# Six of eight modulation blocks as vector sums on VectorE instead of matmuls on TensorE, and a fixed order for the first chunks

## The chip, the cores and the metric

The program runs on one core of one Trainium2 chip. The metric is the time of one execution in device microseconds (us); the median of several executions is given with the lowest and the highest. A profile is one further execution, taken by the hardware profiler.

## The reference

One layer of a diffusion backbone works on 256 latent tokens of width 1024, with 256 context tokens that serve only as keys and values. The part that matters here is the modulation: six vectors of 1024 (shift, scale and gate of two sublayers) come from one matrix of 1024 x 6144, applied to the conditioning vector.

```
mod = (silu(cond) @ w_mod + b_mod)                 # 1 x 6144
sh1, sc1, g1, sh2, sc2, g2 = split(mod, 6)
h = layer_norm(x); hc = layer_norm(ctx)
q, k, v, pool_in, ga, gb = split(modulate(h, sh1, sc1) @ w_in)
y_attn = softmax(q k^T / 8 + bias) v               # keys and values of the context too
y_pool = multiscale_pool(pool_in)
y = (sigmoid(ga) * (y_attn @ w_attn) + sigmoid(gb) * (y_pool @ w_pool)) @ w_out
h = layer_norm(alpha * h + g1 * y)
ffn = hierarchical_moe(modulate(h, sh2, sc2))      # 4 groups x 8 experts, 2 used per token
out = layer_norm(alpha * h + g2 * ffn)
```

modulate(h, sh, sc) is h * (1 + sc) + sh. All inputs are float32. The weights of 32 experts (gate, up and down, 2 MB each) are all streamed.

## The kernel before

**Stages.** The first stage normalises x (tiles xn0, xn1) and the context (xn2, xn3): `spread` (L184) makes a tile's mean and deviation on VectorE and ScalarE, `normalise` (L193) applies them, on VectorE for odd tiles and on ScalarE for even ones. Then a loop over k = 0 to 7 takes one chunk of 128 columns at a time. `modulation(k)` (L215) sums sh1 and sc1 of the chunk for c and for the context's vector: eight matmuls from sil (silu of both vectors) times wm, whose four groups of 32 output rows hold partial sums; VectorE copies them (pms, L226), and `modulation_columns` (L229) adds the four groups with a small matmul on selc, a matrix of ones at every 32nd row. `turn_x` transposes the chunk of xn on TensorE, `modulate` (L247) scales and shifts it on VectorE and splits it by `split` (L67) into a high part (copied on ScalarE) and a low part (subtracted on VectorE). `queries` and `keys` multiply it with split weights: `mm3` (L71) makes three matmuls of each product (high x high, high x low, low x high). So before every weight block, TensorE waits for one low part of VectorE. `wsplit` (L201) is the split of weights.

Then come scores and softmax (`scores` L369, `soft` L380; the softmax is on VectorE and ScalarE), the values (va, weights wvs), attention (po), the pooling branch (ua), the two branch gates (ga, 8 chunks with two halves each, weights wgs), the branch projections (pj, wps), w_out (oa, wos) with LayerNorm and router, and last the 32 experts with their streamed weights.

**Modulation blocks.** The other four vectors g1, sh2, sc2, g2 are columns 2048 to 6143 of w_mod. They are made in eight blocks n = 0 to 7 of 512 columns, two for each vector, scattered over the loops of the later stages. `mod_sum(n)` (L325) loads two tiles of 1 MB (wr), and makes eight matmuls, whose 32-row groups hold partial sums (pr); for g1 and g2 (n = 0, 1, 6, 7) a further matmul puts the bias row from gbt, a part of the tile g2b, in first (L330). ScalarE copies the result to ms. `mod_use` (L346) comes a few steps later in the loops. For n = 0, 1 it sums the groups and spreads them over 128 rows with one matmul (L343; selr is selc widened to 128 columns) into g1b. For n = 2 to 5 it makes columns: four matmuls with a part of ms as weights (L355), every fourth column of it, and VectorE adds biases and makes G2c and B2c, with which the router's weights are scaled (rw, L558, L559). The sums of n = 6, 7 are kept and spread after the router (L666).

In the value loop blocks 0 and 1 stand at k = 2 and 5, in attention blocks 2 and 3, in the gates blocks 4 and 5 at k = 1 and 5 of the first and block 6 at k = 2 of the second, in the projections block 7.

**What sets the order.** All engines work through their own queue in order. A tile scheduler places the instructions of the engines by data and priority, unless `keep_in_program_order` fixes them: `fx` does that for VectorE and ScalarE while early[0] holds, `fp` for TensorE while first[0] holds. All loads of weights go out on SyncE's queue in order, into a ring of eight 1 MB tiles ("big"; wm, wq, wr, wv, wu, wg, wp, wo), and the expert tiles, later also in the memory that earlier stages give back. A load whose tile is still in use holds the queue.

```
def split(hi, lo, src, low=None):
    fx(nc.scalar.copy(hi, src))
    fx((low or V).tensor_sub(lo, src, hi.bitcast(F32)))
```

## Time and profile before

| | before |
|---|---|
| median of 3 runs | 753.5 us (752.71 to 755.31) |
| profiled execution | 753.49 us |
| its span in the trace | 751.9 us |
| TensorE matmul busy | 586.5 us, 78% |
| VectorE busy | 280.4 us, 37% |
| ScalarE busy | 159.8 us, 21% |
| DMA | 260.10 MB, mean 346 GB/s |

The span runs from the first instruction to the last. Busy times are added over each engine and overlap with each other. A share of 78% is an average: which engine or queue limits a stage is seen only in the slices and windows of that stage.

### The profile page before, as it was taken

How to read it: one execution, taken by the hardware profiler on the slowest of the kernel's cores; microseconds unless marked ns; L12 is line 12 of the kernel's file. 1: busy time of each engine (PE TensorE's matmuls, PEld its weight loads, DVE VectorE, ACT ScalarE, POOL GpSimd, SP SyncE). 2: the span in 40 equal slices, each digit the busy share in tenths (PEclk: the TensorE clock that was granted, in tenths of full speed). 3: DMA queues.
4: the chain of work that ended last, by engine and by line, in shares of the span. 5: the costliest groups of instructions: out<-in, count | busy, mean ns of one | idle time of the engine just before them, and what ended most of it. 6: DMA issues, size and time to landing. Idle time of an engine off the chain costs nothing. (4 is left out here: it accounts for less than half of the span.)

```text
span 751.9 us, 16948 instructions
## 1 busy us (share of the span) xinstructions
PE 586.5 (78%) x7477; PEld 434.0 (58%) x7478; DVE 280.4 (37%) x726; ACT 159.8 (21%) x311; POOL 18.1 (2%) x41
## 2 busy tenths in 40 slices
PE   5799999999999998987667667676676576886463
PEld 3688665588899766865345435434443346663352
DVE  4568617633445864533112122112111242321036
ACT  4233435553553553101001001000000000000000
POOL 1000000000000012000000000000000010000003
PEclk8799999999999998999789788696886966989688
DMA  9999464477798874999999999999999999999992
GB/s 293 321 358 385 159 201 169 154 252 265 269 346 331 305 264 177 404 416 414 420 418 418 419 418 419 418 418 418 417 420 418 418 418 416 414 420 418 418 324 84
DMA packets 69629, 260.10 MB, mean 346 GB/s; under 512 B 6569, under 2 KB 27561, under 8 KB 45229
## 3 DMA queue, kind: packets, MB, share of 16 engines
q1 hardware_dynamic: 69550, 258.97, 88.8%
q8 instruction: 60, 0.98, 0.5%
q14 instruction: 19, 0.15, 0.0%
HBM read 257.90 MB, written 1.05 MB: 344 GB/s over the span
## 5 line engine op out<-in xcount | busy, mean ns | idle before, releaser
L752 PE MATMUL gue<-wgu,xgd 128*32 128x128 f32 x4096 | 171.3, 327 | 76.4 <-DMA wgu<-in_w_expert_up_dram 56.8
L752 PEld LDWEIGHTS gue<-wgu,xgd 128*32 128x32 f32 x4096 | 138.2, 131 | 113.6 <-DMA wgu<-in_w_expert_up_dram 68.1
L752 PE MATMUL ye<-wd,aTe 128*32 128x256 f32 x960 | 72.0, 431 | 37.9 <-DVE aTe L814 17.9
L826 DVE TENSOR_TENSOR yp<-ye,g2b 32x256 f32<-32x256 f32 x120 | 50.4, 420 | 88.9 <-PE ye L752 87.6
L803 ACT ACTIVATE sie<-gue 128x128 f32<-128x128 f32 x32 | 8.9, 278 | 329.6 <-PE gue L752 329.6
L809 DVE TENSOR_TENSOR spe<-gue,sie 128x128 f32<-128x128 f32 x32 | 12.0, 376 | 171.5 <-ACT sie L803 171.4
L752 PEld LDWEIGHTS ye<-wd,aTe 128*32 128x32 f32 x960 | 32.1, 120 | 65.5 <-issue 17.4
L752 PE MATMUL pdd<-OHd,hx 128*128 128x128 f32 x256 | 41.7, 312 | 4.1 <-DVE yp L826 3.8
L752 PEld LDWEIGHTS pdd<-OHd,hx 128*128 128x128 f32 x256 | 36.5, 219 | 14.1 <-issue 7.5
L752 PE MATMUL ya<-yp,OTg 128*128 128x512 f32 (+1 forms) x72 | 33.4, 595 | 7.0 <-DVE yp L826 5.8
L780 ACT ACTIVATE xgd<-pdd,B2c,G2c 128x128 f32<-128x128 f32 x32 | 14.7, 458 | 89.3 <-DVE xgd L782 86.7
L782 DVE TENSOR_SCALAR xgd<-pdd,G2c,B2c 128x128 f32<-128x128 f32 x32 | 13.1, 410 | 51.7 <-PE pdd L752 51.5
L752 PEld LDWEIGHTS ya<-yp,OTg 128*128 128x128 f32 x72 | 12.4, 196 | 21.7 <-DVE yp L826 13.9
L336 PE MATMUL pr<-wr,sil 128*32 128x512 f32 x128 | 15.4, 598 | 0.0
L388 ACT ACTIVATE sb<-sb,mx 128x512 f32<-128x512 f32 x16 | 11.4, 717 | 13.3 <-DVE mx L387 13.3
L397 PE MATMUL ptt<-ident,sb 128*128 128x128 f32 x64 | 10.2, 284 | 2.7 <-DVE yaT L69 2.4
L835 DVE COPY OTg<-potg 128x256 f32<-128x256 f32 x8 | 3.4, 425 | 21.2 <-PE ya L752 19.0
L397 PEld LDWEIGHTS ptt<-ident,sb 128*128 128x128 f32 x64 | 6.9, 140 | 6.8 <-DVE yaT L69 4.6
L918 POOL PARTITION_BROADCAST l<-l1r x4 | 2.8, 798 | 318.6 <-DMA wgu<-in_w_expert_up_dram 318.6
L443 PEld LDWEIGHTS po<-pT,kv 128*64 128x64 f32 x128 | 7.2, 136 | 5.6 <-ACT pT L399 2.4
L814 DVE STREAM_TRANSPOSE aTe<-spe 128x128 f32<-128x128 f32 x32 | 10.0, 311 | 1.1
L374 PE MATMUL s<-kv,qT 64*128 64x512 f32 x32 | 9.9, 639 | 0.5 <-DVE mx L386 0.5
(850 smaller groups left out, 977.3 us busy)
## 6 DMA issues: line engine op xcount, KB each, us to landing
wgu<-in_w_expert_gate_dram SPq DMA_DIRECT2D x64, 1024.0 KB, 19.9
wgu<-in_w_expert_up_dram SPq DMA_DIRECT2D x64, 1024.0 KB, 19.9
wd<-in_w_expert_down_dram SPq DMA_DIRECT2D x60, 1024.0 KB, 19.9
wr<-in_w_mod_dram SPq DMA_DIRECT2D x16, 1024.0 KB, 9.1
wm<-in_w_mod_dram SPq DMA_DIRECT2D x16, 512.0 KB, 7.7
wg<-in_w_in_dram SPq DMA_DIRECT2D x8, 1024.0 KB, 5.4
wq<-in_w_in_dram SPq DMA_DIRECT2D x8, 512.0 KB, 8.2
wo<-in_w_out_dram SPq DMA_DIRECT2D x4, 1024.0 KB, 6.5
```

What stands on the lines that cost most here:

```text
L336: nc.tensor.matmul(pm[32 * j:32 * j + 32], lhsT=sil[:, 4 * a + j, :], rhs=w[:, j, :], start=a == 0 and not (gate and j == 0), stop=a == 1, ...
L374: ins = nc.tensor.matmul(ss[r], lhsT=qT[hr, c, P * tt:P * tt + P], rhs=kT[hr, c, :], start=True, stop=True)
L388: nc.scalar.activation(sb, sb, AF.Exp, bias=mx[:, 2:3], scale=1.0, accum_out=mx[:, 3:4])
L397: nc.tensor.transpose(pt[:, P * j:P * j + P], sb[:, P * j:P * j + P], ident)
L443: ins = nc.tensor.matmul(po[64 * r:64 * r + 64, 0:P], lhsT=vr[:, j, 128 * m + 64 * r:128 * m + 64 * r + 64], rhs=pTs[i - 1 + r][:, j, :], ...
L752: return pin(nc.tensor.matmul(*a, **k))
L780: nc.scalar.activation(xg[:, k, :], src, AF.Identity, bias=B2c[:, k:k + 1], scale=G2c[:, k:k + 1])
L782: V.tensor_scalar(xg[:, k, :], src, G2c[:, k:k + 1], B2c[:, k:k + 1], op0=OP.mult, op1=OP.add)
L803: nc.scalar.activation(si, gu[:, 0, :], AF.Silu)
L809: V.tensor_mul(sp.rearrange("p (k r) -> p k r", k=4), by_four(gu[:, 1, :]), by_four(si))
L814: V.transpose(flat(aT), si)
L826: V.tensor_mul(yp[32 * par:32 * par + 32, 256 * d:256 * d + 256], y[32 * d:32 * d + 32, 0:256], g2b[32 * d:32 * d + 32, 256 * d:256 * d + ...
```

## The change

Blocks 0, 1, 4, 5, 6 and 7 are made by the new `mod_half(n, a)`: for each of the two tiles of a block, VectorE multiplies four rows of 512 columns by the partition's own entry of sil and adds them up in ms. The sum over the 128 partitions is then left to the matmuls in `mod_use`, whose other operand is a matrix of ones in place of selr. The biases of the gates are added by VectorE to one row of ms; gbt is loaded by four DMAs to the rows 0, 32, 64 and 96. Blocks 2 and 3 stay in `mod_sum`; ScalarE's copy now stores ms so that the four weight parts are contiguous, and `mod_half` does the same for blocks 4 and 5. The halves stand at k = 1, 2, 4, 5 of the value loop (blocks 0, 1) and of the two gate loops (4, 5 and 6, 7). At the start, `spread` and `normalise` of the context tiles, the splits of the weights of chunks 1 to 3 and the modulation of chunks 1 and 2 get a fixed order, and the loads of chunk 1 go out later.

```diff
--- before.py
+++ after.py
@@ -108,9 +108,7 @@
 
     hrow = [N.tile([P, D], F32, name=f"hrow{i}") for i in range(2)]
     g2b = keep.tile([P, D], F32, name="g2b")
-    gbt, selr = g2b[0:32, 0:512], g2b[:, 512:640]
-    nc.gpsimd.memset(gbt, 0.0)
-    nc.gpsimd.tensor_copy(selr, selc[:, 0:1].to_broadcast([P, P]))
+    gbt = g2b[:, 0:512]
     sil = N.tile([P, KD, 32], F32, name="sil")
     kv = keep.tile([P, 8, 512], F32, tag="k16", name="kv")
     kT, vr = kv[:, 0:4, :], kv[:, 4:8, :]
@@ -213,7 +211,7 @@
     bst = Q.tile([P, H, 6, 64], F32, name="bst")
     qT = Q.tile([P, 4, 256], F32, name="qT")
     def modulation(k):
-        if k:
+        if k > 1:
             load_mod(k)
             load_qk(k)
         wm = wms[k]
@@ -252,14 +250,12 @@
             fx(V.tensor_scalar(hm[:, hs], pt[:, hs], sc[:, 1, j:j + 1], sc[:, 0, j:j + 1], op0=OP.mult, op1=OP.add))
             split(hTs[j][0][:, k, :], hTs[j][1][:, k, :], hm[:, hs])
 
-    def queries(k, ws=None):
-        ws = ws or wsplit(wqs[k][:, k % 2, 0:512], f"wqs{k}")
+    def queries(k, ws):
         for m in range(4):
             mm3(qa[m // 2][:, 256 * (m % 2):256 * (m % 2) + 256], ws, (ALL, slice(P * m, P * m + P)),
                 hTs[0], (ALL, k), k == 0 and m % 2 == 0, k == 7)
 
-    def keys(k, ws=None, js=(0, 1)):
-        ws = ws or wsplit(wqs[k][:, k % 2, 512:1024], f"wks{k}")
+    def keys(k, ws, js=(0, 1)):
         for m in range(4):
             for j in js:
                 mm3(ka[m][:, 256 * j:256 * j + 256], ws, (ALL, slice(P * m, P * m + P)), hTs[j], (ALL, k),
@@ -284,22 +280,34 @@
         fx(V.tensor_sub(ws0[a][1], w0[:, a], ws0[a][0].bitcast(F32)))
     queries(0, ws0[0])
     keys(0, ws0[1], (0,))
-    early[0] = False
-    for i in range(2, 4):
-        normalise(i, spread(i))
+    mv2 = spread(2)
+    mv3 = spread(3)
+    normalise(2, mv2)
+    normalise(3, mv3)
     modulate(0, sc0, (1,))
     keys(0, ws0[1], (1,))
+    load_mod(1)
+    load_qk(1)
+
+    def splits(k):
+        return [wsplit(wqs[k][:, k % 2, 512 * a:512 * a + 512], f"w{k}{a}") for a in range(2)]
+
+    ws = splits(1)
     for k in range(KD):
         if k + 1 < KD:
             p = modulation(k + 1)
             pt = turn_x(k + 1, (0, 1))
         first[0] = False
         if k:
-            queries(k)
+            queries(k, ws[0])
+        old = ws
         if k + 1 < KD:
             modulate(k + 1, modulation_columns(k + 1, *p), (0, 1), pt)
+            if k:
+                ws = splits(k + 1)
         if k:
-            keys(k)
+            keys(k, old[1])
+        early[0] = k < 2
     for i in range(2):
         nc.scalar.activation(flat(qT[:, 2 * i:2 * i + 2, :]), qa[i], AF.Copy, scale=0.125)
     for m in range(4):
@@ -319,40 +327,58 @@
     B2c = keep.tile([P, KD], F32, name="B2c")
     shc = N.tile([P, KD], F32, name="shc")
     scc = N.tile([P, KD], F32, name="scc")
-    nc.sync.dma_start(gbt[0:4], gate_bias)
+    for j in range(4):
+        nc.sync.dma_start(gbt[32 * j:32 * j + 1], gate_bias[j:j + 1])
     sums = []
+
+    def mod_load(n, a):
+        w = big([P, 4, 512], f"wr{n}{a}")
+        nc.sync.dma_start(w, w_mod_k[:, 4 * a:4 * a + 4, 2048 + 512 * n:2560 + 512 * n])
+        return w
 
     def mod_sum(n):
         pm = tmpb(f"pr{n}")
-        gate = n // 2 in (0, 3)
-        if gate:
-            r = n % 2 + n // 6 * 2
-            nc.tensor.matmul(pm[0:32], lhsT=ident[0:32, r:r + 32], rhs=gbt, start=True, stop=False,
-                             skip_group_check=True)
         for a in range(2):
-            w = big([P, 4, 512], f"wr{n}{a}")
-            nc.sync.dma_start(w, w_mod_k[:, 4 * a:4 * a + 4, 2048 + 512 * n:2560 + 512 * n])
+            w = mod_load(n, a)
             for j in range(4):
-                nc.tensor.matmul(pm[32 * j:32 * j + 32], lhsT=sil[:, 4 * a + j, :], rhs=w[:, j, :],
-                                 start=a == 0 and not (gate and j == 0), stop=a == 1, skip_group_check=True)
+                nc.tensor.matmul(pm[32 * j:32 * j + 32], lhsT=sil[:, 4 * a + j, :], rhs=w[:, j, :], start=a == 0,
+                                 stop=a == 1, skip_group_check=True)
         ms = N.tile([P, 512], F32, tag="ms", bufs=2, name=f"ms{n}")
-        nc.scalar.copy(ms, pm)
-        sums.append((n, ms))
-
-    def gate_rows(n, ms, pb, t):
-        nc.tensor.matmul(pb, lhsT=selr, rhs=ms, start=True, stop=True)
-        nc.scalar.copy(t[:, 512 * (n % 2):512 * (n % 2) + 512], pb)
+        nc.scalar.copy(ms.rearrange("q (b p) -> q p b", b=4), pm.rearrange("q (p b) -> q p b", b=4))
+        sums.append((n, ms, True))
+
+    part = {}
+
+    def mod_half(n, a):
+        if a == 0:
+            part[n] = N.tile([P, 512], F32, tag="ms", bufs=2, name=f"ms{n}")
+        ms, w, k = part[n], mod_load(n, a), 4 * a
+        o = ms if n // 2 in (0, 3) else ms.rearrange("q (b p) -> q p b", b=4)
+        for j in range(4):
+            v = w[:, j, :] if n // 2 in (0, 3) else w[:, j, :].rearrange("q (p b) -> q p b", b=4)
+            if k + j == 0:
+                V.tensor_scalar(o, v, sil[:, 0, 0:1], None, op0=OP.mult)
+            else:
+                V.scalar_tensor_tensor(o, v, sil[:, k + j, 0:1], o, op0=OP.mult, op1=OP.add)
+        if a == 0:
+            return
+        if n // 2 in (0, 3):
+            r = 32 * (n % 2 + n // 6 * 2)
+            V.tensor_add(ms[r:r + 1], ms[r:r + 1], gbt[r:r + 1])
+        sums.append((n, ms, False))
 
     def mod_use():
         if not sums or sums[0][0] >= 6:
             return
-        n, ms = sums.pop(0)
+        n, ms, quad = sums.pop(0)
         pb = tmpb(f"pb{n}")
         if n < 2:
-            return gate_rows(n, ms, pb, g1b)
+            nc.tensor.matmul(pb, lhsT=ones, rhs=ms, start=True, stop=True)
+            nc.scalar.copy(g1b[:, 512 * n:512 * n + 512], pb)
+            return
         c = slice(4 * (n % 2), 4 * (n % 2) + 4)
         for b in range(4):
-            nc.tensor.matmul(pb[:, b:b + 1], lhsT=ms.rearrange("q (p b) -> q b p", b=4)[:, b, :], rhs=selc[:, 0:1],
+            nc.tensor.matmul(pb[:, b:b + 1], lhsT=ms[:, P * b:P * b + P], rhs=selc[:, 0:1] if quad else ones[:, 0:1],
                              start=True, stop=True)
 
         def cc(base):
@@ -411,8 +437,8 @@
             wv = big([P, 4, 512], f"wv{k}")
             nc.sync.dma_start(wv, w_in_k[:, k:k + 4, 1024:1536])
         mod_use()
-        if k in (2, 5):
-            mod_sum(k // 3)
+        if k in (1, 2, 4, 5):
+            mod_half(k // 3, k % 3 - 1)
         ws = wsplit(wv[:, k % 4, :], f"wvs{k}")
         for i in range(4):
             mm3(va[i], hTs[i // 2], (ALL, k, slice(P * (i % 2), P * (i % 2) + P)), ws, (ALL, ALL), k == 0, k == 7)
@@ -499,8 +525,8 @@
                     mm3(ga[2 * j + m // 2][:, 256 * (m % 2):256 * (m % 2) + 256], ws,
                         (ALL, slice(P * m, P * m + P)), hTs[0], (ALL, k), k == 0 and m % 2 == 0, k == 7)
             mod_use()
-            if k in ((1, 5), (2,))[b]:
-                mod_sum((4 + k // 5, 6)[b])
+            if k in (1, 2, 4, 5):
+                mod_half(4 + 2 * b + k // 3, k % 3 - 1)
         for i in range(4):
             nc.scalar.activation(flat(sg[b][:, 2 * i:2 * i + 2, :]), ga[i], AF.Sigmoid)
 
@@ -522,8 +548,6 @@
                         (ALL, slice(P * m, P * m + P)), (yaT, ypT)[b], (ALL, k),
                         k == 0 and m % 2 == 0, k == 3)
             mod_use()
-            if k == 1 and b == 0:
-                mod_sum(7)
         if b == 0:
             xas.close()
             ring5 = ctx.enter_context(tc.tile_pool(name="ring5", bufs=1, side="right"))
@@ -661,9 +685,9 @@
 
 
     g2 = []
-    for j, (n, ms) in enumerate(sums):
+    for j, (n, ms, _) in enumerate(sums):
         pb = acc(f"pg{j}")
-        tc.keep_in_program_order(nc.tensor.matmul(pb, lhsT=selr, rhs=ms, start=True, stop=True))
+        tc.keep_in_program_order(nc.tensor.matmul(pb, lhsT=ones, rhs=ms, start=True, stop=True))
         g2.append(pb)
     warm = two("warm")
     for _ in range(3):
```

Three places show what the scheduler makes of it; the names are those of the tiles, with a number that the compiler adds.

The first is the start of VectorE's queue, behind the normalising of the second latent tile; st and mv belong to the context tiles, pms0 is chunk 0's copy. Before:

```order
L196 TENSOR_SCALAR xn1_125<-xn1_125,x1mv_171 128x1024
L187 BN_STATS x2st_234<-xn2_132 128x6 x2
L189 BN_AGGR x2mv_237<-x2st_234 128x2
L187 BN_STATS x3st_243<-xn3_134 128x6
L194 RECIPROCAL x2mv_237<-x2mv_237 128x1
L187 BN_STATS x3st_243<-xn3_134 128x6
L198 SCALAR_TENSOR_TENSOR x2mv_237<-x2mv_237 128x1
L189 BN_AGGR x3mv_246<-x3st_243 128x2
L194 RECIPROCAL x3mv_246<-x3mv_246 128x1
L196 TENSOR_SCALAR xn3_134<-xn3_134,x3mv_246 128x1024
L226 COPY pms0_188<-pm0_179 128x256
```

Now:

```order
L194 TENSOR_SCALAR xn1_123<-xn1_123,x1mv_169 128x1024
L224 COPY pms0_186<-pm0_177 128x256
...
L250 TENSOR_SCALAR hm00_202<-pt00_174,sc0_199 128x256
L69 TENSOR_TENSOR hL_134<-hm00_202,hL_134 128x256
L280 TENSOR_TENSOR w0wlo0_189<-wq0_128,w0whi0_188 128x512
L280 TENSOR_TENSOR w0wlo1_191<-wq0_128,w0whi1_190 128x512
L185 BN_STATS x2st_232<-xn2_130 128x6 x2
L187 BN_AGGR x2mv_235<-x2st_232 128x2
L185 BN_STATS x3st_238<-xn3_132 128x6 x2
```

The copy of chunk 0, its columns and the two low parts of its weights have moved ahead of the statistics of the context tiles.

The second is TensorE's queue in the value loop, between chunks 4 and 5 (weights wvs4, wvs5); wr10 and wr11 are block 1's tiles. Before:

```order
L73 MATMUL va3_890<-wvs4l_979,hC_137 128x512
L73 MATMUL va3_890<-wvs4h_978,hC_137 128x512
L330 MATMUL pr1_994<-g2b_92,ident_69 32x512
L336 MATMUL pr1_994<-wr10_996,sil_95 32x512 x4
L336 MATMUL pr1_994<-wr11_1002,sil_95 32x512 x4
L73 MATMUL va0_887<-wvs5h_1010,hL_136 128x512
```

Now:

```order
L73 MATMUL va3_891<-wvs4l_985,hC_135 128x512
L73 MATMUL va3_891<-wvs4h_984,hC_135 128x512
L73 MATMUL va0_888<-wvs5h_1007,hL_134 128x512
L73 MATMUL va0_888<-wvs5l_1008,hL_134 128x512
...
L73 MATMUL va1_889<-wvs5h_1007,hL_134 128x512
```

The bias matmul and the eight matmuls of block 1 are gone from between the two chunks.

The third is VectorE's queue in the second gate's first chunks, weights wgs100 to wgs110; rw is the router's weights, ms6 and ms7 are blocks 6 and 7. Before:

```order
L69 TENSOR_TENSOR wgs100l_1915<-wg10_1912,wgs100h_1914 128x512
L364 TENSOR_TENSOR scc_844<-pb5_1863,colt_67 128x4
L365 SCALAR_TENSOR_TENSOR G2c_841<-scc_844,colt_67 128x4
L366 SCALAR_TENSOR_TENSOR B2c_842<-scc_844,colt_67 128x4
L558 TENSOR_TENSOR rw_2510<-rw_2510,G2c_841 128x288
L367 TENSOR_TENSOR B2c_842<-B2c_842,shc_843 128x4
L69 TENSOR_TENSOR wgs101l_1931<-wg10_1912,wgs101h_1930 128x512
L559 TENSOR_TENSOR rw_2510<-rw_2510,B2c_842 128x288
L562 TENSOR_REDUCE gb_2517<-rw_2510 128x36 x2
L565 TENSOR_TENSOR gb_2517<-gb_2517,brow_2520 1x36
L69 TENSOR_TENSOR wgs110l_1947<-wg10_1912,wgs110h_1946 128x512
L69 TENSOR_TENSOR wgs111l_1963<-wg10_1912,wgs111h_1962 128x512
```

Now:

```order
L69 TENSOR_TENSOR wgs100l_1908<-wg10_1905,wgs100h_1907 128x512
L362 SCALAR_TENSOR_TENSOR ms6_1971<-wr61_2012,sil_93,ms6_1971 128x512
...
L69 TENSOR_TENSOR wgs101l_1924<-wg10_1905,wgs101h_1923 128x512
...
L392 SCALAR_TENSOR_TENSOR B2c_840<-scc_842,colt_67 128x4
L367 TENSOR_TENSOR ms6_1971<-ms6_1971,g2b_92 1x512
...
L360 TENSOR_SCALAR ms7_2085<-wr70_2086,sil_93 128x512
L582 TENSOR_TENSOR rw_2499<-rw_2499,G2c_839 128x288
L362 SCALAR_TENSOR_TENSOR ms7_2085<-wr70_2086,sil_93,ms7_2085 128x512
L583 TENSOR_TENSOR rw_2499<-rw_2499,B2c_840 128x288
...
L586 TENSOR_REDUCE gb_2506<-rw_2499 128x36
...
L69 TENSOR_TENSOR wgs110l_1940<-wg10_1905,wgs110h_1939 128x512
```

The last steps of block 6 and the first of block 7 stand among the router's products, ahead of wgs110l.

## Rows read from the trace of the kernel before

**Rows 1.** The page, 40 slices of 18.8 us: busy tenths, GB/s.

```profile
PE   5799999999999998987667667676676576886463
...
GB/s 293 321 358 385 159 201 169 154 252 265 269 346 331 305 264 177 404 416 414 420 418 418 419 418 419 418 418 418 417 420 418 418 418 416 414 420 418 418 324 84
```

**Rows 2.** Windows of 10 us: busy of PE, PEld, DVE, ACT, POOL; clock, DMA, GB/s.

```profile
60.00:70.00 10.00, 10.00 (x100) 8.71 (x93) 9.43 (x20) 2.96 (x6) 0.00 (x0) 1.00 1.04 384
...
90.00:100.00 10.00, 10.00 (x46) 6.73 (x48) 1.38 (x2) 1.82 (x3) 0.00 (x0) 1.00 0.67 242
...
130.00:140.00 10.00, 9.03 (x61) 6.71 (x58) 7.01 (x30) 5.62 (x15) 0.00 (x0) 1.00 0.00 0
140.00:150.00 10.00, 9.52 (x77) 5.46 (x75) 5.50 (x19) 5.64 (x13) 0.00 (x0) 1.00 0.81 275
...
170.00:180.00 10.00, 10.00 (x78) 10.00 (x78) 3.66 (x9) 3.44 (x6) 0.00 (x0) 1.00 0.90 319
```

**Rows 3.** Waits of SyncE's queue, 0 to 330 us: total, times, longest (us).

```profile
SPq L495 <- DVE wus7l L69: 22.7, 1, 22.7
...
SPq L862 <- PE pj L73: 13.2, 1, 13.2
```

**Rows 4.** Timeline 0 to 44 us: start, us, engine, line, operation, what it waited for.

```profile
11.18 1.07 PE L223 MATMUL pm<-wm,sil 128*32 128x256 f32 x16
...
13.27 1.28 DVE L187 BATCH_NORM_STATS2 x2st<-xn 128x6 f32<-128x512 f32 x2 [2.41 <-DMA xn<-in_ctx_dram]
...
16.10 1.24 ACT L199 ACTIVATE xn<-xn,x2mv 128x1024 f32<-128x1024 f32 x1 [0.98 <-DVE x2mv L198]
...
17.76 0.81 DVE L196 TENSOR_SCALAR xn<-xn,x3mv 128x1024 f32<-128x1024 f32 x1
18.49 0.41 DVE L226 COPY pms<-pm 128x256 f32<-128x256 f32 x1
...
21.88 1.04 PE L73 MATMUL qa<-hL,w0whi 128*128 128x256 f32 x2 [1.85 <-ACT hL L68]
22.20 1.29 DVE L284 TENSOR_TENSOR w0wlo<-wq,w0whi 128x512 fp32r<-128x512 f32 x2
...
27.80 0.63 PE L244 MATMUL pt<-ident,xn 128*128 128x128 f32 x2
```

**Rows 5.** Timeline of TensorE around block 1, 98 to 102 us.

```profile
98.47 1.04 PE L330 MATMUL pr<-g2b,ident 32*32 32x512 f32 x2
99.44 1.92 PE L336 MATMUL pr<-wr,sil 128*32 128x512 f32 x16
101.30 0.50 PE L73 MATMUL va<-wvs5h,hL 128*128 128x512 f32 x1
```

**Rows 6.** Timeline of TensorE: two column sums with their neighbours.

```profile
37.64 0.50 PE L231 MATMUL pm<-selc,pms 128*128 128x2 f32 x4
...
133.23 1.92 PE L355 MATMUL pb<-selc,ms 128*128 128x1 f32 x8
135.08 1.13 PE L374 MATMUL s<-kv,qT 64*128 64x512 f32 x4
```

**Rows 7.** VectorE groups by shape, 0 to 300 us; the last from the page.

```profile
L390 DVE TENSOR_SCALAR sb<-sb,mx 128x512 f32<-128x512 f32 x16 | 7.7, 484 | 0.4
...
L606 DVE SCALAR_TENSOR_TENSOR hrow<-hrow,oa 128x512 f32<-128x512 f32 x4 | 2.7, 684 | 0.1
...
L69 DVE TENSOR_TENSOR yaT<-po,yaT 128x128 fp32r<-128x128 f32 x8 | 2.3, 289 | 0.0
...
L809 DVE TENSOR_TENSOR spe<-gue,sie 128x128 f32<-128x128 f32 x32 | 12.0, 376 | 171.5 <-ACT sie L803 171.4
```

**Rows 8.** Timeline of SyncE and of TensorE: a tile of block 5.

```profile
141.54 0.96 SPq L334 DMA_DIRECT2D wr<-in_w_mod_dram  x1
...
183.17 1.92 PE L336 MATMUL pr<-wr,sil 128*32 128x512 f32 x16
```

**Rows 9.** The page, DMA issues: KB each, median us to landing.

```profile
wr<-in_w_mod_dram SPq DMA_DIRECT2D x16, 1024.0 KB, 9.1
```

## Prediction, made before the changed kernel was run

> **What bounds the kernel now.** I read the slices of the page first, then windows, then the waits of the DMA queue, then the start of the timeline. The slices [rows 1] show two regimes. Up to slice 15, some 300 us, TensorE is busy 9 tenths or more nearly everywhere and HBM traffic goes up and down, between 154 and 385 GB/s; from slice 16 on traffic stands at 404 to 420 GB/s to the last slices while TensorE has room. So the expert half is bound by the transfers, and the first half by something else. Windows say what: in 130 to 140 us nothing is transferred at all while TensorE is busy 9.03 of 10 us [rows 2], so the transfers are not what the first half waits for. The waits of SyncE's queue say what the transfers wait for: a ring tile that TensorE or VectorE has not yet given back, 22.7 us for the last read of wu and 13.2 us for a matmul of the branch projections, after which the first expert tiles go out [rows 3]. I therefore take it that a microsecond taken off TensorE's path before 300 us lets the expert stream start a microsecond earlier; its bytes and rate stay, and so the end moves by the same. That carry of one to one is a choice; what speaks for it is that the slices hold 404 GB/s or more from slice 16 to slice 37 [rows 1]: the stream fills once and never thins before its end.
>
> **The start.** The columns of chunk 0 are summed on TensorE by 12.25 us (11.18 and 1.07), but VectorE copies them only at 18.49, because the statistics and the normalising of the context tiles stand before the copy on its queue, from 13.27 to 18.57; the first query matmul follows at 21.88 [rows 4]. The order now puts the copy first. It can run at about 12.5, 6.0 us earlier, and the first query matmul at about 15.9. The context work does not vanish: it now stands behind the two subtractions of 1.29 us, which move from 22.20 to about 16.2 and end at 17.5. From there the context block takes 5.3 us as it did, or about 4.2, since in the new order ScalarE's second square root no longer waits behind a 1.24 us normalise; its end is 21.7 to 22.8. TensorE's context transposes, now at 27.80, then start at 21.8 to 22.9: 4.9 to 6.0 us earlier. I take 5.4. What is late next is the splitting of the weights of chunks 1 to 3: they were made whenever VectorE had room, and now stand in a fixed order behind the modulation of the same chunk, with the low parts last. That makes each step's first low part about half a microsecond late on TensorE in two steps: 1.0 lost. Start: **4.4 us**, ends 2 and 6.
>
> **Six blocks leave TensorE.** A block holds TensorE from 99.44 to the next value matmul at 101.30, 1.86 us, and a gate block's bias matmul from 98.47 to 99.44, 0.97 us [rows 5]. By the code there are eight blocks, and a bias for 0, 1, 6 and 7. Blocks 0, 1, 4, 5, 6 and 7 go, 2 and 3 stay: 6 x 1.86 = 11.2 us, and 4 x 0.97 = 3.9 us for the biases. Six ScalarE copies of the sums go too; nothing waits on ScalarE there, so they count nothing.
>
> **The column sums.** Blocks 2 to 5 are read as weights with a step of four elements; 8 records take from 133.23 to 135.08, 1.85 us [rows 6]. The sums are now stored so that each weight is contiguous. The nearest row with contiguous weights and a narrow moving side has 4 records in 0.50 us [rows 6], so 8 cost 1.0. Four times 0.85 is 3.4; two of the four lie in attention, where part may be hidden, and I take **3.0** (0 to 3.4).
>
> **What VectorE gets.** Per block one TENSOR_SCALAR and seven SCALAR_TENSOR_TENSOR of 128x512. The trace has both: 484 ns from SBUF, and 684 ns [rows 7]. A block is 0.48 + 7 x 0.68 = 5.3 us, six are 32 us, and four bias additions of one row by 512 are at most 4 x 0.68 = 2.7 us: 35 us on an engine that nobody waits for as long as it has room. It has: busy 1.38 of 10 us in the value stage and 3.66 in the gate stage [rows 2]. Blocks 5 to 7 add 16 us over about 50 us there, some 3 per 10, and so about 7 in 10. The cover is thin in two places. Block 0 begins where VectorE was busy 9.43 of 10 us [rows 2], and its last four steps stand between the first softmax steps and the low part of value chunk 2: about a microsecond on TensorE. In the gates the last steps of block 6 and the first of block 7 stand with the router's products ahead of the low part wgs110l, as the order shows: by counting rows, VectorE gets there 0.7 us after TensorE. With the last softmax pair, which now has four steps of block 4 in front of it, I charge **2.0 us** for all collisions; ends 0 and 12, the latter a third of the 35 us.
>
> Two more edits cost nothing. The gate bias goes as four DMAs of 2 KB instead of one, on a queue whose loads run far ahead of use; without that cover it would be a few tenths of a microsecond for each issue. And a block's two halves are now on SyncE's queue a step apart, and wpa goes behind wg16. A block's first step on VectorE waits for its tile, and behind it are queued the low parts that TensorE waits for; but the loads have a long lead. A tile of block 5 goes out at 141.54 and is used at 183.17 [rows 8].
>
> Sum: 4.4 + 11.2 + 3.9 + 3.0 - 2.0 = 20.5 us. The profiled execution took 753.49 us, 1.6 more than its span and equal to the median of the runs within 0.01. 753.5 - 20.5 gives **733.0 us**. On the ends of the terms, 2 + 11.2 + 3.9 + 0 - 12 = 5 and 6 + 15.1 + 3.4 - 0 = 24.5: 748 and 729.
>
> [...] Blocks 4 and 5 write and reread their sums in steps of 512 bytes, and no row shows VectorE doing that. The nearest pair: a product of 128 columns that reads with a step of 16 bytes takes 376 ns, a subtraction of as many contiguous columns 289 ns [rows 7], 87 more. Over 512 columns that is 0.35 us, over 16 steps 5.6 us, on a stretch (140 to 165 us) where VectorE is busy 5.5 of 10 us at the start [rows 2] and gets 10.6 us of new work anyway, so it would be near full. I charge none of it, since TensorE first reads wgs000l well after the last softmax, and keep it as a rival. [...]
>
> **Rivals.**
> - *VectorE sets the pace* in the value and gate stages, a third of its new work lands on TensorE: 733.0 + 12 - 2 = 743. For it: the two thin places. Against it: 1.38 and 3.66 busy of 10 [rows 2]. Chance 0.12.
> - *Strided steps are slow* and VectorE is full where blocks 4 and 5 stand: 733.0 + 5.6 = 738.6. Chance 0.08.
> - *The start gains nothing*: the context chain, or the late low parts of chunks 1 to 3, eat it: 733.0 + 4.4 = 737.4. For it: TensorE's next work needs just that chain [rows 4]. Chance 0.10.
> - *Slower*: VectorE's queue stops on a block's tile. If a ring tile for blocks 5, 6 and 7 comes free only as VectorE gets to it, each of them holds the low parts for a landing, median 9.1 us [rows 9]: 3 x 9.1 = 27, and 733.0 + 27 = 760. It decides from a hold of 7 us each. Against it: the lead of 41 us [rows 8]. Chance 0.05.
> - *No carry*: TensorE gets ahead and the expert stream starts no sooner, by a wait not seen here: 753. Against it: the waits [rows 3]. Chance 0.03.
>
> **The numbers.** The forecast itself has 0.62 and its own range is 729 to 737. With the strided and the start case, 0.80, the range is 728 to 742. A measurement of this kernel can tell about 0.3%, 2.3 us, from no change: faster 0.62 + 0.12 + 0.08 + 0.10 = 0.92, the same 0.03, slower 0.05.
>
> **What would show it.** In the changed kernel's timeline: chunk 0's copy at 12 to 13 us, the context transposes at 22 to 23; no bias matmul, 32 records of the block matmul instead of 128; column sums of about 1.0 us; VectorE at 7 in 10 in the gates with TensorE still at 10; the slice in which traffic reaches 400 GB/s about one slice earlier, and the last expert tile landing about 20 us earlier. I am wrong if TensorE shows idle time ended by VectorE's low parts or its ms steps, if VectorE's idle time is ended by DMAs of wr, or if the prefix is 20 us shorter and the end is not.

## The result, and the profile after

The changed kernel takes 732.77 us in the median of 4 runs (731.51 to 733.88), the kernel before 753.68 beside it: a ratio of 0.9729, with a 95% interval of 0.9706 to 0.9751. That is 20.9 us less; the forecast was 733.0, in a range of 728 to 742. The profiled execution took 733.38 us, with a span of 731.7.

The page of the changed kernel: busy time by engine, the 40 slices (of 18.3 us here) and the group of the new steps.

```profile
PE 570.9 (78%) x7373; PEld 429.5 (59%) x7374; DVE 316.5 (43%) x778; ACT 156.1 (21%) x305; POOL 17.4 (2%) x39
...
PE   7898999999999989885767756668576659757462
...
GB/s 292 309 347 386 270 176 158 265 312 349 354 309 312 261 157 385 416 417 418 419 418 420 417 419 420 417 418 417 419 417 419 420 415 417 416 418 419 418 311 70
...
L362 DVE SCALAR_TENSOR_TENSOR ms<-wr,sil,ms 128x512 f32<-128x512 f32 x42 | 36.9, 878 | 0.2
```

They answer to [rows 1]: TensorE works 570.9 us instead of 586.5, and traffic is at 385 GB/s in slice 15, where it was 177, and at 416 in slice 16. The slice in which traffic passes 400 GB/s is still slice 16. The 42 SCALAR_TENSOR_TENSOR steps on VectorE take 878 ns in the mean, not 684. On SyncE's queue the two waits of [rows 3] are still there, 1.0 and 3.0 us shorter (again total, times, longest):

```profile
SPq L521 <- DVE wus7l L69: 21.7, 1, 21.7
...
SPq L886 <- PE pj L73: 10.2, 1, 10.2
```

So the transfers still wait for TensorE and VectorE to give tiles back, only sooner, as the forecast took it.

The start, timeline of the changed kernel; to be read against [rows 4]:

```profile
10.83 1.07 PE L221 MATMUL pm<-wm,sil 128*32 128x256 f32 x16
...
11.97 0.42 DVE L224 COPY pms<-pm 128x256 f32<-128x256 f32 x1 [2.07 <-PE pm L221]
...
14.97 1.04 PE L73 MATMUL qa<-hL,w0whi 128*128 128x256 f32 x2 [1.85 <-ACT hL L68]
...
20.96 0.69 PE L242 MATMUL pt<-ident,xn 128*128 128x128 f32 x2
```

Chunk 0's copy runs at 11.97 instead of 18.49, the first query matmul at 14.97 instead of 21.88, and the context transposes at 20.96 instead of 27.80.

To see where time went I compare the start of the same matmul in both traces; the difference is called the lead.

| start of | before | after | lead, us |
|---|---|---|---|
| first query matmul | 21.88 | 14.97 | 6.9 |
| queries of chunk 5 | 61.22 | 54.34 | 6.9 |
| scores | 77.85 | 73.26 | 4.6 |
| transposes of the softmax (end of the value stage) | 110.52 | 101.09 | 9.4 |
| first gate's first weights (end of attention) | 156.96 | 146.05 | 10.9 |
| second gate's first weights | 192.72 | 176.76 | 16.0 |
| projections | 218.78 | 200.09 | 18.7 |
| w_out | 245.41 | 223.70 | 21.7 |
| assignment of the tokens (pc) | 284.87 | 264.07 | 20.8 |
| span | 751.9 | 731.7 | 20.2 |

The lead grows where a block left TensorE, and falls in two places: from 6.9 to 4.6 between chunk 5 and the scores, and by 0.9 between w_out and pc; behind pc another 0.6 is lost. What happens at the first of them, on VectorE and then on TensorE:

```profile
52.38 0.42 DVE L69 TENSOR_TENSOR hL<-hm,hL 128x256 fp32r<-128x256 f32 x1
55.32 1.23 DVE L322 TENSOR_TENSOR hrow<-xn,gb 128x1024 f32<-128x1024 f32 x1 [2.52 <-DMA gb<-in_rows_dram]
56.47 0.42 DVE L69 TENSOR_TENSOR hC<-hm,hC 128x256 fp32r<-128x256 f32 x1
...
57.27 0.61 PE L229 MATMUL pm<-selc,pms 128*128 128x2 f32 x4 [1.27 <-DVE pms L224]
...
68.80 0.50 PE L73 MATMUL qa<-hL,w70h 128*128 128x256 f32 x2 [1.26 <-ACT hL L68]
```

hC is chunk 5's context part; its low part must be there before the keys. Between hL and hC the product of the residual rows (hrow) stands in VectorE's queue, and it waits 2.52 us for the landing of the broadcast rows gb. TensorE is idle for 1.27 us until the copy of chunk 6's sums (pms), which stands behind hC, and for 1.26 us more ahead of chunk 7's queries. In the kernel before, the product stood one step later, behind hC, started 4.7 us later and waited for nothing:

```profile
60.06 1.22 DVE L314 TENSOR_TENSOR hrow<-xn,gb 128x1024 f32<-128x1024 f32 x1
```

VectorE in four of the windows of [rows 2], and in 80 to 90 us (columns as there):

```profile
60.00:70.00 10.00, 8.39 (x77) 7.40 (x77) 9.25 (x21) 3.28 (x7) 0.00 (x0) 1.00 1.04 385
...
80.00:90.00 10.00, 10.00 (x43) 7.80 (x43) 9.35 (x22) 4.39 (x9) 0.00 (x0) 1.00 0.64 219
90.00:100.00 10.00, 10.00 (x44) 7.88 (x43) 3.54 (x5) 1.47 (x4) 0.00 (x0) 1.00 1.01 315
...
140.00:150.00 10.00, 9.86 (x70) 8.15 (x70) 9.18 (x14) 5.42 (x12) 0.00 (x0) 1.00 0.77 279
...
170.00:180.00 10.00, 10.00 (x86) 9.95 (x84) 9.69 (x20) 7.27 (x12) 0.00 (x0) 1.00 1.02 397
```

It is busy more than 9 of 10 us in four of the five, beside TensorE at 8.39 to 10; the first of them was so before (9.43).

### The profile page after: what moved, and what is told of

It is laid out like the page before. It is cut to its first block, busy times and chain, and to the rows that moved or that the text cites. A ratio compares the mean times of both kernels' runs of the same rounds, so it can differ in the third digit from the quotient of the medians.

```text
span 731.7 us, 16776 instructions
## 1 busy us (share of the span) xinstructions
PE 570.9 (78%) x7373; PEld 429.5 (59%) x7374; DVE 316.5 (43%) x778; ACT 156.1 (21%) x305; POOL 17.4 (2%) x39
## 4 chain that ended last, share of the span: by engine, by line
DMA 52%; issue 36%; PE 8%; DVE 3%; POOL 0%; DVEq 0%; ACT 0%; SPq 0%; POOLq 0%
DMA wgu<-in_w_expert_up_dram 28%; DMA wd<-in_w_expert_down_dram 17%; DMA wgu<-in_w_expert_gate_dram 8%; PE gue L776 4%; PE ye L776 1%; PE pdd L776 1%; PE ya L776 1%; DVE yp L1058 0%; DVE se L684 0%; PE yl L776 0%; DVE fst L1066 0%; DVEq L1172 0%; DVE fin L1090 0%; DVE eq L684 0%; DVE spe L833 0%
## 5 line engine op out<-in xcount | busy, mean ns | idle before, releaser
L776 PE MATMUL gue<-wgu,xgd 128*32 128x128 f32 x4096 | 173.3, 329 | 82.5 <-DMA wgu<-in_w_expert_up_dram 52.5
L776 PE MATMUL ye<-wd,aTe 128*32 128x256 f32 x960 | 73.3, 435 | 32.7 <-DVE aTe L838 15.7
L362 DVE SCALAR_TENSOR_TENSOR ms<-wr,sil,ms 128x512 f32<-128x512 f32 x42 | 36.9, 878 | 0.2
L804 ACT ACTIVATE xgd<-pdd,B2c,G2c 128x128 f32<-128x128 f32 x32 | 14.6, 457 | 84.3 <-DVE xgd L806 80.7
## 6 DMA issues: line engine op xcount, KB each, us to landing
wgu<-in_w_expert_up_dram SPq DMA_DIRECT2D x64, 1024.0 KB, 20.5
```

Of the source, the lines that this page charges most:

```text
L362: V.scalar_tensor_tensor(o, v, sil[:, k + j, 0:1], o, op0=OP.mult, op1=OP.add)
L776: return pin(nc.tensor.matmul(*a, **k))
L804: nc.scalar.activation(xg[:, k, :], src, AF.Identity, bias=B2c[:, k:k + 1], scale=G2c[:, k:k + 1])
```

## The experiments

**The parts of the change by themselves.** The first run, e1_start, has the fixed order of the start alone; the second, e2_blocks, everything but that; the third, e3_cols, the contiguous column sums alone.

```diff
 # e1_start: before, with the new start
-        if k:
+        if k > 1:
             load_mod(k)
...
-    early[0] = False
-    for i in range(2, 4):
-        normalise(i, spread(i))
+    mv2 = spread(2)
+    mv3 = spread(3)
...
 # e3_cols: before, with mod_sum's copy
-        nc.scalar.copy(ms, pm)
+            nc.scalar.copy(ms.rearrange("q (b p) -> q p b", b=4), pm.rearrange("q (p b) -> q p b", b=4))
...
-lhsT=ms.rearrange("q (p b) -> q b p", b=4)[:, b, :]
+lhsT=ms[:, P * b:P * b + P]
```

> The kernel before with the fixed order of the first chunks alone; all eight blocks stay on TensorE. Theory (each microsecond that TensorE gains before the expert stream arrives at the end): in the changed kernel the first query matmul is 6.9 us earlier, but the scores only 4.6, 1.0 of it the bias matmul of block 0, which stood ahead of them; so 3.6 to 4.6 us, about 749.5. The forecast had 4.4. If the rival on the start holds (it gains nothing at the end), 753.5. The view that tells: in the fifth to seventh chunk VectorE should wait some 2.5 us for the landing of the broadcast rows gb, and the lead should fall there from 6.9 to below 5.

> The changed kernel with the old order of the first chunks: the six blocks on VectorE and the contiguous sums alone. If the parts add, 732.8 and the 3.6 to 4.6 us of the start: about 737. If the start and the blocks take the place of each other (VectorE's work in the value stage finds room only because the start is earlier, or the other way round), either under 735 or over 740.

> The kernel before with contiguous column sums alone: ScalarE stores the sums of blocks 2 to 5 so that each weight is contiguous. Theory: four times 0.85 us off TensorE, up to 3.4 us at the end: 750.1 to 751.5. If two of the four are hidden in attention, 751.8. If weights with a step cost TensorE nothing here, or ScalarE's store with a step holds it, 753.5 or more.

Measured: the start alone 748.65 us against 753.34 (ratio 0.9952, 0.9932 to 0.9972; its twelve runs lie between 745.74 and 753.39); everything else alone 737.05 (0.9782, 0.9761 to 0.9802); the sums alone 748.73 (0.9940, 0.9919 to 0.9960). The start and the rest add up: 0.9952 x 0.9782 is 0.9735, the whole change 0.9729. In the start's own trace the lead is 7.5 us at the first query and 4.4 at the scores, and it stays 4.4 down to the first expert's matmuls; the loss is at the same place, with a longer wait:

```profile
54.77 1.23 DVE L324 TENSOR_TENSOR hrow<-xn,gb 128x1024 f32<-128x1024 f32 x1 [2.78 <-DMA gb<-in_rows_dram]
```

The sums alone gain more than the forecast gave them. Timeline of that run, the place that answers to [rows 6]:

```profile
133.45 0.95 PE L358 MATMUL pb<-selc,ms 128*128 128x1 f32 x8
134.33 1.13 PE L377 MATMUL s<-kv,qT 64*128 64x512 f32 x4
```

From the first sum to the next matmul it is 0.88 us instead of 1.85; the lead grows by 0.97 at each of the four, those in attention too, 3.9 in all, and none of it is given back down to pc.

**The matmuls put back beside VectorE's work.**

```diff
 # e6_both: after, in mod_half; nothing reads px
+        px = tmpb(f"px{n}{a}")
         for j in range(4):
+            nc.tensor.matmul(px[32 * j:32 * j + 32], lhsT=sil[:, k + j, :], rhs=w[:, j, :], start=True, stop=True)
```

> The changed kernel, and TensorE makes the matmuls of the six blocks too, into a tile that nothing reads; VectorE's work is the same. It prices the matmuls apart from everything else. Theory (one to one to the end): 6 x 1.86 = 11.2 us more, 744.0. Rival (no carry, TensorE has slack somewhere before the expert stream): 732.8 to 738.

Measured: 747.32 us, 14.6 more than the changed kernel's median; its profiled execution took 744.96, the lowest of its seven runs and 11.6 more than that of the changed kernel. The lead over the changed kernel falls by 1.1 to 1.2 us at nearly each of the twelve half blocks, and from the scores, where it is 1.1 ahead, to the projections, where it is 11.9 behind, by 13.0. No slack swallows it, and the first expert matmul starts 11.6 us later. Of the rival "no carry" nothing is left; why the median shows 3 us more than the trace stays open.

**VectorE's room, used up on purpose.** Behind each of the 48 steps stands one more, which adds zero times the same row.

```diff
 # e5_double: after, in mod_half
+            V.scalar_tensor_tensor(o, v, zeros[:, 0:1], o, op0=OP.mult, op1=OP.add)
```

> The changed kernel with one more step on VectorE behind each of the 48, which adds zero times the same row: 48 steps of 0.74 to 1.13 us, some 42 us more on VectorE and nothing on TensorE. If VectorE still has the room that the forecast spoke of, 732.8 to 736. If the room is used up (from 60 to 190 us the changed kernel leaves VectorE 23 us idle, and in the value stage only 8 for 12 more), 10 to 20 us come out: 743 to 753.

Measured: 753.31 us (ratio to the kernel before 1.0005, 0.9990 to 1.0021): the whole gain is gone. Windows of this run:

```profile
90.00:100.00 10.00, 5.90 (x14) 3.65 (x13) 10.00 (x16) 0.88 (x2) 0.00 (x0) 0.66 0.75 217
...
180.00:190.00 10.00, 6.49 (x45) 5.78 (x44) 9.64 (x12) 4.10 (x6) 0.00 (x0) 0.93 0.65 222
...
210.00:220.00 10.00, 7.53 (x50) 7.53 (x51) 9.94 (x17) 2.69 (x5) 0.00 (x0) 0.83 0.87 309
```

In these three windows VectorE stands at 9.6 to 10 of 10, and TensorE falls to 5.9, 6.5 and 7.5; in other windows with VectorE as full TensorE keeps 8.9 to 10. At the projections this run is 21.7 us behind the changed kernel: 6.9 come from the value stage, and 13 from the last chunk of the first gate on. So half of the 42 us came out on TensorE and half found room: the cover that the forecast counted on is real, and in these two stretches it is spent. Not all of the 21.7 us need be waiting for VectorE, since the granted clock is down there too (0.66, 0.93 and 0.83, third column from the right); the two were not parted.

**Blocks 2 and 3 on VectorE too.**

```diff
 # e8_eight: after, in attention
-        if m == 1:
-            mod_sum(2 + tt)
+        if m in (1, 2):
+            mod_half(2 + tt, m - 1)
```

> The changed kernel with blocks 2 and 3 on VectorE too, in attention. TensorE loses 2 x 1.86 = 3.7 us of work; VectorE gets 16 strided steps, some 18 us, where it is 7.7 to 9.6 of 10 busy (110 to 140 us of the changed kernel). If VectorE now sets the pace of attention: its 7 us of room there are used and 10 land on TensorE, 732.8 - 3.7 + 10, 737 to 740. If TensorE still does: 729.

Measured: 736.46 us (ratio 0.9787, 0.9768 to 0.9806), 3.7 slower than the changed kernel and just below the 737 to 740 expected. Windows:

```profile
100.00:110.00 10.00, 6.45 (x44) 4.46 (x42) 9.96 (x15) 5.36 (x11) 0.00 (x0) 1.00 0.79 276
...
130.00:140.00 10.00, 9.27 (x57) 5.88 (x57) 9.96 (x32) 6.50 (x16) 0.00 (x0) 1.00 0.46 144
```

TensorE is at 6.45 of 10 where VectorE is at 9.96; in the changed kernel it is 9.74 and 6.18 in the same window. In attention VectorE has no room for two more blocks, and six do better than eight. The trace alone would not show it: the profiled execution is the lowest of the five (733.32 us), 2.1 us behind the changed kernel at the first gate and with the same span.

**The strided steps of blocks 4 and 5.** First with plain stores and TensorE reading with a step; then with plain steps and one copy into column order on ScalarE for each block.

```diff
 # both
-        o = ms if n // 2 in (0, 3) else ms.rearrange("q (b p) -> q p b", b=4)
+        o = ms
-            v = w[:, j, :] if n // 2 in (0, 3) else w[:, j, :].rearrange("q (p b) -> q p b", b=4)
+            v = w[:, j, :]
...
 # e4_plain alone
-lhsT=ms[:, P * b:P * b + P]
+lhsT=ms[:, P * b:P * b + P] if quad else ms.rearrange("q (p b) -> q b p", b=4)[:, b, :]
...
 # e10_act alone
+            nc.scalar.copy(mp.rearrange("q (b p) -> q p b", b=4), ms.rearrange("q (p b) -> q p b", b=4))
```

> The changed kernel with blocks 4 and 5 stored contiguously by VectorE and read by TensorE with a step again. It prices VectorE's strided steps: in the changed kernel they take 1.13 us instead of 0.74, so VectorE is spared 14 x 0.39 and 2 x 0.33, about 6 us, and TensorE pays twice the 0.97 us that the run with contiguous sums alone showed for each sum. If the strided steps are off the path (the forecast): 732.8 + 1.9, less up to 1.0 of the stalls seen beside block 5, so 733.7 to 734.7. If they are on it (the rival on strided steps): 732.8 + 1.9 - 6, about 729.

> The changed kernel with blocks 4 and 5 summed contiguously on VectorE and put into column order by one copy each on ScalarE. In the run with plain stores the gate stage's stalls beside blocks 4 and 5 gave back 1.7 us and the reads with a step took 1.9. Here only the first should be left: 1.7 less, 731.1, if the strided steps are what stalls TensorE; 732.8 if it is their number.

Two steps of the changed kernel, of block 0 and of block 4:

```profile
77.72 0.74 DVE L362 SCALAR_TENSOR_TENSOR ms<-wr,sil,ms 128x512 f32<-128x512 f32 x1
```

```profile
136.97 1.16 DVE L362 SCALAR_TENSOR_TENSOR ms<-wr,sil,ms 128x512 f32<-128x512 f32 x1
```

A step of block 4 reads the weights as they lie, but rereads and writes its sum at a stride of 512 bytes; it takes 1.16 us instead of 0.74. The plain stores give 733.09 us (0.9752, 0.9729 to 0.9775): no difference. The trace has both halves of why: from the end of the value stage to chunk 3 of the first gate this run makes up 1.74 us on the changed kernel, and then pays about 1.0 twice, as its column sums take 1.91 us again:

```profile
163.39 1.91 PE L381 MATMUL pb<-ones,ms 128*128 128x1 f32 x8
```

With ScalarE's copy only the gain is left: from 0.40 us behind at the end of the value stage to 1.16 ahead in the first gate. The time, 733.23 us (0.9713, 0.9690 to 0.9736), does not show it apart from the changed kernel's: its five runs differ by more (730.58 to 733.74). In the profiled one TensorE's granted clock was at 0.50 from 23.6 to 27.0 us (the 16 matmuls of chunk 1's sums took 1.94 us there, 1.07 in the changed kernel), chunk 1 started 0.9 us later, and the landing of gb varies too (below). So by the two traces, one execution each, the strided steps cost some 1.6 us, not the rival's 5.6 and not nothing.

**The wait for gb.** First the residual products are fixed behind the last chunk's copy; then gb is loaded earlier and they are fixed behind the copies of chunks 5 and 6, the first of them some steps ahead of where it was.

```diff
 # both
-        fx(V.tensor_copy(flat(pms), pm[:, 0:256]))
+        tc.keep_in_program_order(V.tensor_copy(flat(pms), pm[:, 0:256]))
...
 # e7_hrow
-        V.tensor_mul(hrow[i], xn[i], gin)
-        V.tensor_add(hrow[i], hrow[i], bin_)
+        tc.keep_in_program_order(V.tensor_mul(hrow[i], xn[i], gin))
+        tc.keep_in_program_order(V.tensor_add(hrow[i], hrow[i], bin_))
 # e9_gb, in the loop over the chunks
+            if k == 3:
+                gb = [N.tile([P, D], F32, tag=f"bc{i}", name=f"gb{i}") for i in range(2)]
+                for i, t in enumerate(gb):
+                    nc.sync.dma_start(t, rows[:, D * i:D * i + D].to_broadcast([P, D]))
...
+        if k in (4, 5):
+            h = hrow[k - 4]
+            tc.keep_in_program_order(V.tensor_mul(h, xn[k - 4], gb[0]))
+            tc.keep_in_program_order(V.tensor_add(h, h, gb[1]))
```

> The changed kernel with the four products and sums of the residual rows (hrow) fixed behind the copy of the last chunk's sums on VectorE, so that no low part of a chunk stands behind the landing of the broadcast rows gb. If that wait is what the lead lost between the fourth chunk and the scores (6.9 to 4.6 us), 732.8 - 2.3, about 730.5. If the 4.9 us of this work only hold the first softmax and the low parts of the value stage instead, 732.8 or a little more.

> The changed kernel with the broadcast rows gb loaded five loads earlier and the four residual products fixed behind the copies of chunks 5 and 6 on VectorE. VectorE has the same work at nearly the same place; only the wait for the landing goes. If that wait is what the lead lost between chunk 4 and the scores: 732.8 less 2 to 3, about 730.3, and lead 6.9 kept to the scores. If VectorE's work itself holds the chunks there: 732.8, with the loss in the same place and no idle time for gb.

Moved behind the chunks, the products make it worse, 735.97 us (0.9761, 0.9742 to 0.9780): more than the second expectation's "a little more", in the place that it named. The scores come 3.4 us earlier than in the changed kernel, and then all of it and 3.5 more is lost in the value stage, where block 0's steps and the products meet:

```profile
70.00:80.00 10.00, 9.93 (x36) 5.83 (x36) 9.40 (x28) 5.42 (x10) 0.00 (x0) 1.00 0.78 271
80.00:90.00 10.00, 6.01 (x13) 3.81 (x12) 10.00 (x22) 1.71 (x5) 0.00 (x0) 0.67 0.70 235
```

```profile
84.32 0.79 PE L73 MATMUL va<-wvs2l,hL 128*128 128x512 f32 x1 [3.99 <-DVE wvs2l L69]
```

TensorE waits 3.99 us for the low part of value chunk 2, and its granted clock is down behind it (0.67 in 80 to 90 us). With gb early the time is **728.43 us** (0.9650, 0.9628 to 0.9673), 4.3 below the changed kernel's median and apart from its interval; no kernel of this study is faster. The first product now follows chunk 5's copy at once, at 48.72, the second chunk 6's:

```profile
55.00 0.42 DVE L224 COPY pms<-pm 128x256 f32<-128x256 f32 x1
55.33 1.22 DVE L317 TENSOR_TENSOR hrow<-xn,gb 128x1024 f32<-128x1024 f32 x1
```

The lead over the changed kernel is 3.3 us at the scores and 4.5 from the end of the value stage to w_out. Over the kernel before it is 6.8 us at chunk 5 and, with the bias's 1.0, 7.9 at the scores: nothing is lost on the way.

The wait and the loss go together over the profiles. From the queries of chunk 5 to the scores it takes, in us (0.97 taken off where block 0's bias matmul stands between them):

| run | wait for gb | chunk 5 to scores |
|---|---|---|
| before, e2_blocks, e3_cols | none | 15.7, 15.5, 15.7 |
| e9_gb, e12_all | none, gb early | 15.5, 15.5 |
| e7_hrow | none, products moved away | 15.4 |
| e11_late | 0.44 | 15.5 |
| e6_both | 1.37 | 17.8 |
| e10_act | 2.05 | 18.5 |
| e8_eight | 2.16 | 18.6 |
| after | 2.52 | 18.9 |
| e5_double | 2.60 | 20.1 |
| e1_start | 2.78 | 19.0 |
| e4_plain | 3.47 | 21.0 |

The product is one and the same, and where its wait is short (e11_late, in the same order as the changed kernel) nothing is lost: so it is the wait and not VectorE's work. In e6_both, e10_act, e8_eight and the changed kernel chunk 5 itself, from its queries to chunk 6's, loses the wait less 0.6 us (0.8 to 1.9), and another 1.5 us are lost from there to the scores, which e11_late does not lose; why was not followed up. In e4_plain and e5_double TensorE's granted clock was at 0.50 right behind the wait (58.3 to 61.7 and 58.9 to 62.3 us; a matmul of 256 columns took 0.41 us there, 0.28 ahead of it and behind it), and their rows hold that too.

**Blocks 0 and 1 later, and all together.**

```diff
 # e11_late: after, in the value loop; e12_all has the edits of e9_gb, e10_act and e11_late
-        if k in (1, 2, 4, 5):
-            mod_half(k // 3, k % 3 - 1)
+        if k >= 4:
+            mod_half(k // 2 - 2, k % 2)
```

> The changed kernel with blocks 0 and 1 at chunks 4 to 7 of the value loop in place of 1, 2, 4 and 5: away from the stretch of 60 to 90 us, where VectorE is 9.3 of 10 busy, into 85 to 105 us, where it is 3.5 to 6.2 busy. In the changed kernel the lead loses only some 0.2 us of its 5.7 beside block 0. If VectorE's queue at block 0 is nearly harmless: 732.6 to 732.8. If the steps now meet the softmax's end at 100 us, up to 5 us more: 735 to 738.

> All three together: rows gb early, blocks 4 and 5 put into order by ScalarE, blocks 0 and 1 late. If the three terms add: 732.8 - 2.5 - 1.7, about 728.6. If the late blocks cost what the plain order did not: 730 to 734.

Measured: 730.16 us (0.9681, 0.9656 to 0.9706) and 728.52 us (0.9662, 0.9637 to 0.9686). The late blocks look faster than the changed kernel, but the profile of that run had a wait for gb of only 0.44 us, and its lead, 2.2 at the scores, is 3.3 at the end of the value stage and 3.2 in the gates: the moved blocks themselves are worth about 1 us there. Whether the other five runs had a short wait is not known. All three together come out at the 728.6 that was expected, but gb early alone does so too: the terms do not add. The traces show a part of why. From the scores to the transposes of the softmax it takes 27.8 us in the changed kernel, 26.6 with gb early, 26.7 with the late blocks and 27.9 with both, so in the value stage each alone gains what the two together do not; and in the profiled execution of e12_all the granted clock was at 0.50 from 23.6 to 27.1 us, as in e10_act, and chunk 1 started 0.9 us later than in e9_gb.

## Why the prediction was right, by its own steps

- **What bounds the kernel, and the carry of one to one**: shown. Work put back on TensorE (e6_both) and taken from it (e3_cols, e2_blocks) comes out at the end nearly in full, and traffic is at 385 GB/s in slice 15, where it was 177. In a single execution the distance to the changed kernel changes by up to 1.5 us between the projections and the end, and by 3.3 in e4_plain (last section).
- **The start**, forecast 4.4 as 5.4 less 1.0: the gain was larger, 6.9 at the first query and still 6.9 at chunk 5, and nothing was lost in chunks 1 to 3. Chunk 0's copy ran at 11.97 and not at 12.5, the first query matmul 3.0 us behind it and not 3.4. The step that failed is the sentence that the low parts of chunks 1 to 3 are late next; what was late next was the landing of gb, which took back 3.3 us ahead of the scores (6.9 and the bias's 1.0, less 4.6). Alone the start is worth 3.6 us by the ratio (1 - 0.9952 of 753.3), 4.4 by the lead in its trace and 4.7 by the medians.
- **Six blocks**, forecast 11.2 and 3.9: the lead grows by 2.0 us at blocks 4 and 5 and by 3.0 at blocks 1, 6 and 7 with their biases, so 12.2 and 3.9. The term was a little small: it was taken up to the next matmul's start, and the first matmuls of the next chunk lost 0.1 to 0.2 us more.
- **The column sums**, forecast 3.0: 3.9. Mis-sized: 0.97 each in place of 0.85, and nothing hidden in attention.
- **The collisions on VectorE**, forecast 2.0: the start without the bias that the table counts in it (4.6 - 1.0), 16.1 for the blocks and 3.9 for the sums make 23.6, and the lead at w_out is 21.7: 1.9 were lost. The size was right, the places only in part. The one that was named, wgs110l, shows in the timeline of the changed kernel:

```profile
180.19 0.39 PE L73 MATMUL ga<-hL,wgs110l 128*128 128x256 f32 x1
```

Its matmul starts 0.55 us after the one ahead of it (179.64), and the lead falls by 0.3, not 0.7. The other 1.6 lie beside blocks 4 and 5, at the strided steps, which the forecast charged at nothing. A step took 0.74 us plain and 1.16 strided, where 0.68 and 1.03 were reckoned; so the stride of 512 bytes cost 0.42 us a step, more than the rival's 0.35, and most of it was covered.
- **VectorE's room** was reckoned too large. The new steps took 43 us and not 35 (36.9 for the 42 steps, 3.5 for the six first ones, 2.7 for the biases), and VectorE was busy 8.2 of 10 us from 140 to 200 us, up to 9.77 in one window, where the forecast's sign had 7 in 10. TensorE's busy time there stays at 9.3 to 10 all the same. The forecast's sign of being wrong, idle time of TensorE ended by VectorE's low parts or its ms steps, is absent from the value and gate stages; ahead of the scores TensorE's idle time is ended by VectorE's copy pms, held up by gb, and by ScalarE's hL.
- **The sum**: 20.5 was forecast, and 20.8 is the lead behind the router, 20.2 at the end of the span. That the sum comes so near is partly luck, as errors of both signs met: 0.8 too much at the start, 1.0 and 0.9 too little at the blocks and the sums, and 0.9 lost to TensorE's clock in the router, which no step had.
- **The rival that VectorE sets the pace** was the nearest: twice its new work costs the whole gain. The rival on the start was half right: something did eat a part of it, but neither of the two that it named. The slower rival (tiles that hold VectorE's queue) did not show: ahead of its 42 steps VectorE was idle for 0.2 us in all, and ahead of the six first ones for none.

## What to carry to other kernels

Before a chain is moved earlier, look on its engine's queue for work that waits for a transfer whose landing does not move: what was late enough to be hidden becomes the wait. When work is given to an idle engine, count its room stage by stage in windows; 8 us of 10 free in one stage do not help a stage that has one. Run a version with the suspected cost doubled: it tells how much cover is left, which a good result does not.

## What the runs showed of the hardware that was not expected

The wait for one transfer (gb) was 0.44 to 3.47 us in eight profiles whose loads ahead of it are the same. Two things make it up: the landing, at 54.20 to 55.86, and the time at which VectorE comes to the product, at 51.99 to 54.05, late in e10_act and e11_late, whose granted clock was at 0.50 again from 23.6 and 22.6 us on (a matmul of 256 columns took 0.41 us there, and 0.28 in the changed kernel, at 1.00). A difference of a few microseconds between two kernels that both have this wait was therefore read from the stages of the traces, not from the medians alone.

TensorE's clock fell in the router, and not in each kernel at the same place. Windows of 1 us, before, after, and in e6_both (columns as in [rows 2]; PEclk is the third from the right):

```profile
276.00:277.00 1.00, 1.00 (x9) 1.00 (x10) 0.35 (x3) 1.00 (x1) 0.00 (x0) 1.00 0.93 393
...
278.00:279.00 1.00, 1.00 (x3) 0.24 (x1) 0.92 (x11) 1.00 (x2) 0.00 (x0) 0.50 1.01 426
```

```profile
252.00:253.00 1.00, 0.24 (x2) 0.27 (x3) 1.00 (x4) 0.20 (x1) 0.00 (x0) 1.00 0.89 172
...
254.00:255.00 1.00, 0.84 (x4) 0.84 (x5) 0.32 (x2) 1.00 (x3) 0.00 (x0) 0.50 0.97 401
...
259.00:260.00 1.00, 1.00 (x2) 0.20 (x2) 1.00 (x1) 1.00 (x2) 1.00 (x1) 0.50 1.04 385
```

```profile
264.00:265.00 1.00, 0.35 (x3) 0.38 (x4) 1.00 (x3) 0.09 (x1) 0.00 (x0) 1.00 0.58 147
...
266.00:267.00 1.00, 0.95 (x9) 0.95 (x9) 0.32 (x2) 1.00 (x2) 0.00 (x0) 1.00 1.01 426
```

TensorE had been busy 0.24 of 1 us in 252 to 253 of the changed kernel; from 254 to 260 the clock is at 0.50. In the kernel before it was at 0.50 from 278 to 280, with 0.75 in the microsecond ahead and 0.54 in the one behind; there TensorE had been busy 0.33 of the microsecond from 275. In e6_both the clock stayed at 1.00 in each window from 262 to 270, where TensorE had been busy 0.35 of the microsecond from 264. The eight logits matmuls fall into it in the changed kernel and take 1.92 us; in the kernel before they run at 1.00, in 1.08 us. So they end 0.9 us later. What decides it was not tried.

The same clock also counts behind the router. From 268 to 274 us, at the first expert's matmuls, it is at 0.50 in the changed kernel and at 1.00 in e4_plain: 50 of them take 3.20 us in the one and 1.72 in the other. There e4_plain goes from 1.5 us behind to 1.5 ahead, and its span ends 1.5 us earlier although it was 1.85 behind at the projections.
